# A one-core transformer layer with an expert feed-forward: more expert tiles computed ahead of the dense stage, and four smaller moves in the order of its engines

## The chip, the cores and the metric

The kernel runs on one core of a Trainium2 chip. The metric is the device time of one execution in microseconds (us). Three runs of the kernel before gave 1698.33, 1704.1 and 1705.66 us; their median, 1704.1 us, is the time before. The engines are named as in the profile: PE is TensorE (matmuls), PEld its weight load, DVE is VectorE, ACT is ScalarE, POOL is GpSimd, SP is SyncE, which issues transfers.

## The reference, cut to what matters

One layer works on 512 latent tokens of width 1024. Differential attention gives `h`, a layer norm of the residual follows, and then comes a product-key expert network with 16384 experts:

```
h = layer_norm(DN_ALPHA * h + g1 * o, ln_g[0], ln_b[0])
u = h * (1 + sc2) + sh2
q = (u @ w_q).reshape(T, 8, 2, 128)              # 8 heads, 2 halves
s = einsum('thcd,ckd->thck', q, sub_keys)        # key scores, 128 keys per half
s1, i1 = top_k(s[:, :, 0], 16);  s2, i2 = top_k(s[:, :, 1], 16)
top_s, pos = top_k(all 256 sums s1 + s2, 16)     # the 16 chosen experts idx of each head
g = softmax(top_s)
act = gelu(einsum('thkd,td->thk', u_tab[idx], u))
f = einsum('thk,thkd->td', g * act, v_tab[idx])
h = layer_norm(DN_ALPHA * h + g2 * f, ln_g[1], ln_b[1])
```

## The kernel before, in words

Tokens stand in four blocks of 128. Blocks 0, 1 and 2 (`DT = 3`) are computed densely: all 16384 experts are taken, as 128 tiles of 128 experts, and an expert that a token did not choose gets the gate 0. Block 3 is computed sparsely: the 128 chosen rows of `u_tab` and the 128 chosen rows of `v_tab` of each token are gathered by POOL and multiplied up on DVE (`fetch`, `gather`, `some`). All large products are float32 by three matmuls: each operand is split by ACT into a rounded part (`hi`) and by DVE or POOL into the rest (`lo`), and `mm3` issues hi·hi, hi·lo and lo·hi (lines 146, 148 and 149).

From the product-key part on, the stages are these.

- **Key scores** (`scores`): 16 rounds. Each splits one block of `w_q` (`qhi` on ACT, `qlo` on POOL), multiplies it with `u` (24 matmuls), multiplies with the keys (4 matmuls), and DVE takes the top 16 of four blocks (`top16`). In the last round there is no product, and one expert tile is computed instead.
- **Choices** (`choose`, `decide`): for each block DVE finds the 16 best of the sums, turns positions into expert numbers, and the softmax of the gates takes one exponential (`gg`) on ACT, line 961. Blocks 3, 0 and 1 come here one after the other. In between, PE computes expert tiles ahead: `ahead(n, rows)` splits a tile of `u_t` (`split_up`: `ur` is loaded by SP, `uhi` is made on ACT, `ulo` on POOL), makes 24 matmuls over blocks 0 to 2 (`up`, tile `a`), and ACT takes the GELU of them into `at`; `ad` in DRAM holds the results until they are needed. Splits run up to three tiles ahead of the matmuls. `rows` of the sparse block are gathered beside them; three of these stay `HOLD`-en before DVE uses them.
- **Gates** (`onehot`, `gates`): for each of the blocks 0 to 2, eight steps. DVE builds one-hot tiles `o`, `oh`, `ol`, 32 small matmuls spread the gates over all experts, ACT copies them to `w`, SP stores them in DRAM (`gd`). Each step also computes two expert tiles ahead (`WITH_GATES`), with `ulo` on DVE. The choice of block 2 stands behind the eight steps of block 0.
- **Dense stage** (`down`): for each of the 128 tiles `prepare` loads `v_t` (`vr`, two tiles in one transfer on ACT's queue), the stored `at` (`ar`) and gates (`gq`), and splits them: `vh`, `wh` on ACT, `vl`, `w`, `wl` on DVE; 18 matmuls add the tile to six accumulators. `prepare` runs two tiles ahead. Tiles that were not computed ahead ("fresh" ones) get their `up` here, six tiles before their use. At its end the rows of block 3 are complete and `finish` makes the last norm; for that `residual` loads the normalized state `nd`, and POOL multiplies with `ln_g` and adds `ln_b` (lines 1221 and 1222). Blocks 0 to 2 are finished after the last five tiles.

The order on each engine is that of a scheduler, which may move an instruction when it is free to, except for what goes through `Pinned` (`self.V`, `self.A`, `self.T`): those stand in the order of the program, and in the profile they all have line 97. `SPILL = 44` makes 90 tiles computed ahead. `WITH_CHOICE` lists by block how many tiles stand beside its choice, and how many gathered rows: (9, 0) for block 3, (9, 5), (11, 6), (9, 5) for blocks 0, 1, 2.

Of the kernel before, what the change touches and what calls it, by code (L numbers as in the profile page):

```python
# [31 lines left out]
SPILL = 44  # L32


WITH_CHOICE = {DT: (9, 0), 0: (9, 5), 1: (11, 6), 2: (9, 5)}
# [67 lines left out]
class Net:  # L103
# [5 lines left out]
    def build(self):  # L109
        with ExitStack() as es:  # L110
# [6 lines left out]
            self.T = Pinned(self, self.nc.tensor)  # L117
            self.consts()
# [539 lines left out]
    def mix(self):  # L658
# [8 lines left out]
        self.nd = self.dram.tile([NT, 128, D], F32, name="nd")  # L667
        self.keys = self.u2p.tile([128, 2, 128], F32, name="keys")
# [182 lines left out]

# [3 lines left out]
    def scores(self):  # L855
# [4 lines left out]
        with tc.tile_pool(name="qp", bufs=1, reuse_waits="tile") as qp:  # L860
# [17 lines left out]
            def split(k):  # L878
                if k < 2 * H:
                    S[k] = [qp.tile([128, KB, 128], FR, name=x, bufs=2) for x in ("qhi", "qlo")]  # L880
                    self.A.activation(S[k][0], RAW[k], AF.Copy)
                    (nc.vector if k < 4 else nc.gpsimd).tensor_tensor(S[k][1], RAW[k], S[k][0].bitcast(F32), op=OP.subtract)  # L882
# [11 lines left out]
            for k in range(2 * H):  # L894
# [4 lines left out]
                elif k:  # L899
                    self.ahead(1)  # L900
                ps = self.bank()
# [7 lines left out]
                if k == 1:  # L909
# [8 lines left out]
                    self.ug = tc.alloc_tile_pool(name="ug", bufs=1, side="right", reuse_waits="tile")  # L918

# [16 lines left out]
    def decide(self, t, h0, h1):  # L936
# [24 lines left out]
        self.A.activation(g, g, AF.Exp)  # L961
# [27 lines left out]
        V.tensor_reduce(by_head(self.i2f), m, axis=AX.X, op=OP.add)  # L989
        yield 1  # L990
# [140 lines left out]
    def down(self):  # L1131
# [7 lines left out]
        def prepare(j, at_end=None):  # L1139
# [14 lines left out]
            self.hi_lo(vh, vl, vq[j // 2][:, j % 2])  # L1154
# [3 lines left out]
            nc.vector.tensor_tensor(w.rearrange("p (q t) -> p q t", t=32), gq[j // 8][:, :, j % 8],  # L1158
                                    self.AT[j // 2][:, j % 2].rearrange("p (q t) -> p q t", t=32), op=OP.mult)
            self.prepared = self.hi_lo(wh, wl, w)  # L1160
# [3 lines left out]
        for j in fresh:  # L1164
            if j < AHEAD:
                self.up(j)
        prepare(0)
        prepare(1)
# [11 lines left out]
        for j in range(128 - TM):  # L1180
            if at(j - 1) == 256 and not row:
                row += self.last_rows()
                skip[DT] = self.residual(self.ag.tile([128, D], F32, name="gr", bufs=5), DT, row)
# [14 lines left out]
        for t in range(DT):  # L1198
            skip[t] = self.residual(fp.tile([128, D], F32, name="h", bufs=3), t, row)
# [9 lines left out]
    def last_rows(self):  # L1209

        row = []
        for n in range(4):
# [104 lines left out]
```

## Time and profile before

| what | value |
|---|---|
| runs of the kernel before | 1698.33, 1704.1, 1705.66 us |
| time of the profiled execution | 1702.72 us |
| its span, first to last instruction | 1700.9 us |
| mean granted TensorE clock | 0.98 of full speed |
| busy: PE, DVE, ACT, POOL | 1608.8, 1462.5, 761.8, 646.2 us |
| moved by DMA | 435.92 MB, 256 GB/s on average |

The product-key part begins at about 425 us of the span, the choices at 528 us, the first gates at 683 us, the last gates end at 963.7 us, the first dense step starts at 992.5 us. A busy share says how long an engine had work in it, not whether the work was on the path that ended last; what counts here is where PE stood idle, and for whom it waited. In a row of the waits, "PE v L146 <- ACT wh L138: 9.8, 2, 8.8" is read as: the matmuls of line 146 into tile `v` waited for ACT's tile `wh` (line 138), 9.8 us in total, twice, 8.8 us at most. In a timeline row the brackets hold the idle time of the engine just before, and who ended it. Rows of stretches give, for each engine, busy time and (in brackets) the number of instructions, then the granted clock, the busy share of the DMA engines, and GB/s.

### The profile page before, as it was taken

Reading aid. Unit: us, or ns where it says so; the run is one execution under the profiler, and the core shown is the slowest. Engines: PE = TensorE matmul, PEld = TensorE weight load, DVE = VectorE, ACT = ScalarE, POOL = GpSimd, SP = SyncE. Lnnn points to the kernel's source line nnn. Section 1 sums busy time; section 2 is a strip of 40 time slices with the busy share of each in tenths; the row PEclk is TensorE's granted clock in tenths of the full one; section 3 lists DMA queues with packets and bytes.
Section 4 is the critical chain, followed back from the end, with each engine's and each line's share of the span. In section 5 each row is a group of like instructions: output and inputs, shape, how many; then the busy total and the mean of one; then the engine's idle time right before and its main releaser. Section 6 shows DMA issues by size and latency. Waiting matters only on the chain.

```text
span 1700.9 us, 24498 instructions
## 1 busy us (share of the span) xinstructions
PE 1608.8 (95%) x9057; PEld 1430.2 (84%) x9057; DVE 1462.5 (86%) x2598; ACT 761.8 (45%) x1148; POOL 646.2 (38%) x368
## 2 busy tenths in 40 slices
PE   7899999997999999899999979999999999999977
PEld 3788897876888998899999968888888888888865
DVE  6688897887799999999999468989899789888978
ACT  5475656654333343564666533333333333333322
POOL 1000000000234676327333235655566556655552
PEclk9999999998999999899999989999999999999988
DMA  8765746403222566798999999989899889988952
GB/s 317 192 173 153 180 130 177 151 21 127 89 86 73 177 224 206 266 347 266 333 367 340 331 359 360 378 319 374 322 376 360 336 331 372 362 333 296 356 193 97
DMA packets 134920, 435.92 MB, mean 256 GB/s; under 512 B 13200, under 2 KB 38288, under 8 KB 123408
## 3 DMA queue, kind: packets, MB, share of 16 engines
q1 hardware_dynamic: 75328, 201.02, 34.7%
q0 software_dynamic: 36864, 134.23, 21.2%
q10 hardware_dynamic: 22608, 99.10, 16.6%
q8 instruction: 71, 1.16, 0.3%
q14 instruction: 49, 0.40, 0.1%
HBM read 372.57 MB, written 47.05 MB: 247 GB/s over the span
## 4 chain that ended last, share of the span: by engine, by line
PE 77%; DVE 9%; DMA 6%; issue 4%; ACT 2%; POOL 2%; SPq 0%; ACTq 0%; DVEq 0%; POOLq 0%
PE v L149 11%; PE v L146 10%; PE v L148 10%; PE a L149 10%; PE a L146 10%; PE a L148 9%; PE v L97 3%; PE qkv L146 2%; PE qkv L149 2%; PE qkv L148 2%; DMA adw<-in_ada_b_dram 2%; PE sc L409 2%; DMA qs<-kh 1%; PE mp L228 1%; POOL ulo L1019 1%
## 5 line engine op out<-in xcount | busy, mean ns | idle before, releaser
L146 PE MATMUL a<-u2h,uhi 128*128 128x384 f32 x1024 | 346.7, 339 | 4.5 <-ACT at L97 2.8
L149 PE MATMUL a<-u2h,ulo 128*128 128x384 f32 x1024 | 344.9, 337 | 6.2 <-POOL ulo L1019 4.5
L148 PE MATMUL a<-u2l,uhi 128*128 128x384 f32 x1024 | 343.9, 336 | 0.0
L146 PE MATMUL v<-vh,wh 128*128 128x512 f32 x768 | 300.9, 392 | 9.8 <-ACT wh L138 9.8
L148 PE MATMUL v<-vl,wh 128*128 128x512 f32 x768 | 301.7, 393 | 8.1 <-DVE vl L139 8.1
L149 PE MATMUL v<-vh,wl 128*128 128x512 f32 x768 | 301.7, 393 | 4.6 <-DVE wl L139 4.5
L1095 POOL DMA_INDIRECT gr<-in_peer_u_dram,eidx x128 | 184.3, 1440 | 242.4 <-DVE gr L1104 226.6
L1019 POOL TENSOR_TENSOR ulo<-ur,uhi 128x1024 fp32r<-128x1024 f32 x79 | 210.2, 2666 | 124.2 <-ACT uhi L97 70.1
L138 ACT ACTIVATE vh<-vr 128x1024 fp32r<-128x1024 f32 x128 | 134.6, 1054 | 237.6 <-DMA vr<-in_v_t_dram 96.7
L1095 POOL DMA_INDIRECT gr<-in_peer_v_dram,eidx x128 | 183.1, 1431 | 150.0 <-DVE facc L1111 129.8
L139 DVE TENSOR_TENSOR vl<-vr,vh 128x1024 fp32r<-128x1024 f32 x128 | 164.5, 1286 | 70.6 <-ACT vh L138 70.6
L882 POOL TENSOR_TENSOR qlo<-qraw,qhi 128x1024 fp32r<-128x1024 f32 x12 | 28.8, 2401 | 465.2 <-ACT qhi L97 465.2
L149 PEld LDWEIGHTS a<-u2h,ulo 128*128 128x128 f32 x1024 | 193.2, 189 | 8.5 <-POOL ulo L1019 6.5
L146 PEld LDWEIGHTS a<-u2h,uhi 128*128 128x128 f32 x1024 | 193.3, 189 | 7.1 <-ACT at L97 3.7
L148 PEld LDWEIGHTS a<-u2l,uhi 128*128 128x128 f32 x1024 | 193.4, 189 | 1.5
L1111 DVE SCALAR_TENSOR_TENSOR facc<-gr,act,facc 128x1024 f32<-128x1024 f32 x127 | 184.6, 1453 | 6.1 <-DMA gr<-in_peer_v_dram,eidx 6.1
L146 PEld LDWEIGHTS v<-vh,wh 128*128 128x128 f32 x768 | 145.4, 189 | 39.9 <-ACT wh L138 10.5
L148 PEld LDWEIGHTS v<-vl,wh 128*128 128x128 f32 x768 | 145.6, 190 | 38.6 <-DVE vl L139 8.8
L149 PEld LDWEIGHTS v<-vh,wl 128*128 128x128 f32 x768 | 145.3, 189 | 36.5 <-DVE wl L139 5.9
L97 ACT ACTIVATE at<-a 128x384 f32<-128x384 f32 x90 | 44.2, 492 | 184.7 <-PE a L149 111.3
L139 DVE TENSOR_TENSOR wl<-w,wh 128x384 fp32r<-128x384 f32 x128 | 93.1, 728 | 23.9 <-ACT wh L138 23.5
L138 ACT ACTIVATE wh<-w 128x384 fp32r<-128x384 f32 x128 | 65.1, 517 | 106.7 <-PE v L148 65.7
(269 smaller groups left out, 3257.4 us busy)
## 6 DMA issues: line engine op xcount, KB each, us to landing
ur<-in_u_t_dram SPq DMA_DIRECT2D x128, 512.0 KB, 5.8
vr<-in_v_t_dram ACTq DMA_DIRECT2D x64, 1024.0 KB, 8.2
gq<-gd SPq DMA_DIRECT2D x16, 1536.0 KB, 12.3
gd<-w SPq DMA_DIRECT2D x12, 1920.0 KB, 8.9
ad<-at SPq DMA_DIRECT2D x45, 384.0 KB, 6.3
ar<-ad SPq DMA_DIRECT2D x45, 384.0 KB, 7.3
adw<-in_ada_b_dram ACTq DMA_DIRECT2D x64, 256.0 KB, 3.5
wraw<-in_w_qkv_dram ACTq DMA_DIRECT2D x21, 512.0 KB, 4.2
```

The lines of the kernel that those rows point to most:

```text
L97: ins = getattr(self.engine, name)(*args, **kwargs)
L138: (hi_engine or nc.scalar).activation(hi, src, AF.Copy)
L139: return (lo_engine or nc.vector).tensor_tensor(lo, src, hi.bitcast(F32), op=OP.subtract)
L146: ins = nc.tensor.matmul(out, lh, rh, start=first and i == 0, stop=False)
L148: nc.tensor.matmul(out, lh, rl, start=False, stop=False)
L149: ins = nc.tensor.matmul(out, ll, rh, start=False, stop=last and i == n - 1)
L228: nc.tensor.matmul(mp[:2, 2 * i + n], l[:, kb], r[:, ns], start=kb == 0 and k == 0, stop=kb == KB - 1 and k == 2)
L409: nc.tensor.matmul(ps[:, c, n0:n1], QS[h, c][:, v, t * 128:(t + 1) * 128], KS[h, c][:, n0:n1], start=v == 0, stop=v == 1)
L882: (nc.vector if k < 4 else nc.gpsimd).tensor_tensor(S[k][1], RAW[k], S[k][0].bitcast(F32), op=OP.subtract)
L1019: self.paced = (lo_engine or self.nc.gpsimd).tensor_tensor(lo, raw, hi.bitcast(F32), op=OP.subtract)
L1095: ins = nc.gpsimd.indirect_dma_start(out=self.GR[n], out_offset=None, in_=a["peer_v"] if n >= K else a["peer_u"], in_offset=bass.IndirectO ...
L1111: ins = nc.vector.scalar_tensor_tensor(self.facc, r, self.act[:, k:k + 1], self.facc, op0=OP.mult, op1=OP.add)
```

## The change

Five things are edited.

1. `SPILL` goes from 44 to 48: the formula in `spilled` now picks 98 tiles to compute ahead, and 30 are left fresh in the dense stage (38 before). `WITH_CHOICE` becomes (10, 0), (11, 3), (14, 3), (9, 3): one, two and three tiles more beside the choices of blocks 3, 0 and 1, and five rows less by the end of block 1, two less beside block 2. Five tiles instead of three are left over behind the last gates; 199 instead of 192 rows are left to the dense stage.
2. The exponential of each choice is issued later on ACT: after the expert numbers are complete instead of right after the differences are formed. Two tiles' GELUs and splits that stood behind it now stand ahead.
3. The splits of the first three tiles are issued in rounds 13, 14 and 15 of the key scores instead of all in round 15 (`split_ahead`).
4. `prepare(0)` and `prepare(1)` are pinned on DVE and ACT, as are tiles of `up` ahead of them (none is there with either value of `SPILL`).
5. `residual` no longer multiplies and adds. Rounds 5 to 12 of the key scores do that on POOL, in one step a round, each behind the round's `qlo`; rounds 3, 5, 7 and 9 load `nd`, and POOL's own queue writes the result to `hd`. The end loads `hd`. `qlo` is pinned on POOL from tile 4 on, so that these steps stand between.

```diff
-SPILL = 44
-WITH_CHOICE = {DT: (9, 0), 0: (9, 5), 1: (11, 6), 2: (9, 5)}
+SPILL = 48
+WITH_CHOICE = {DT: (10, 0), 0: (11, 3), 1: (14, 3), 2: (9, 3)}
...
+            self.P = Pinned(self, self.nc.gpsimd)
...
     def ahead(self, n, rows=0, lo_engine=None):
-        for i in range(n):
-            while len(self.ready) < min(self.done + 3, len(self.early)):
-                j = self.early[len(self.ready)]
-                self.ready.append(self.split_up(j, self.A, lo_engine))
+        for i in range(min(n, len(self.early) - self.done)):
+            self.split_ahead(self.done + 3, lo_engine)
...
+    def split_ahead(self, n, lo_engine=None):
+        while len(self.ready) < min(n, len(self.early)):
+            self.ready.append(self.split_up(self.early[len(self.ready)], self.A, lo_engine))
...
-                    (nc.vector if k < 4 else nc.gpsimd).tensor_tensor(S[k][1], RAW[k], S[k][0].bitcast(F32), op=OP.subtract)
+                    (nc.vector if k < 4 else self.P).tensor_tensor(S[k][1], RAW[k], S[k][0].bitcast(F32), op=OP.subtract)
...
+                if k > 2 * H - 4:
+                    self.split_ahead(k - 2 * H + 4)
...
+                    row, skip = self.rows(0), []
+                if 3 <= k < 13:
+                    t, step = divmod(k - 5, 2)
+                    if k in (3, 5, 7, 9):
+                        skip.append(self.ag.tile([128, D], F32, name="gr", bufs=5))
+                        nc.sync.dma_start(skip[-1], self.nd[len(skip) - 1])
+                    if k > 4:
+                        self.P.tensor_tensor(skip[t], skip[t], row[step], op=(OP.mult, OP.add)[step])
+                        if step:
+                            self.P.dma_start(self.hd[t], skip[t])
...
         V.tensor_tensor(g, top, top[:, :, 0:1].to_broadcast([128, N, TK]), op=OP.subtract)
         yield 1
-        self.A.activation(g, g, AF.Exp)
...
         V.tensor_reduce(by_head(self.i2f), m, axis=AX.X, op=OP.add)
+        self.A.activation(g, g, AF.Exp)
         yield 1
...
-        prepare(0)
-        prepare(1)
+        prepare(0, vector=self.V, act=self.A)
+        prepare(1, vector=self.V, act=self.A)
...
-    def residual(self, h, t, row):
-        nc = self.nc
-        nc.sync.dma_start(h, self.nd[t])
-        nc.gpsimd.tensor_tensor(h, h, row[0], op=OP.mult)
-        nc.gpsimd.tensor_tensor(h, h, row[1], op=OP.add)
+    def residual(self, h, t):
+        self.nc.sync.dma_start(h, self.hd[t])
         return h
```

How this moves instructions is read from the built programs at three places. The first is ACT in the choice of block 3; `uhi` is the split of an expert tile, `at` its GELU, `gg` the exponential, and a table load stands at each change between GELU and exponential. Before:

```order
L97 ACTIVATE uhi_5588<-ur_5586 128x1024
L97 ACTIVATE at_5549<-a_5592 128x384
L97 ACTIVATE uhi_5622<-ur_5620 128x1024
L97 ACTIVATE at_5626<-a_5627 128x384
L97 ACT_TABLE_LOAD
L97 ACTIVATE gg_4497<-gg_4497 128x128
L97 ACTIVATE uhi_5665<-ur_5663 128x1024
L97 ACT_TABLE_LOAD
L97 ACTIVATE at_5626<-a_5669 128x384
```

The same place now:

```order
L97 ACTIVATE uhi_5689<-ur_5687 128x1024
L97 ACTIVATE at_5651<-a_5693 128x384
L97 ACTIVATE uhi_5722<-ur_5720 128x1024
L97 ACTIVATE at_5726<-a_5727 128x384
L97 ACT_TABLE_LOAD
L97 ACTIVATE gg_4498<-gg_4498 128x128
L97 ACTIVATE uhi_5769<-ur_5767 128x1024
L97 ACT_TABLE_LOAD
L97 ACTIVATE at_5726<-a_5773 128x384
```

The neighbours look alike; what moved is the count ahead of `gg`: five GELUs of expert tiles (one from the key scores, four of this choice) before, seven now.

The second is ACT at the start of the dense stage; the first `vr` holds tiles 0 and 1 of `v_t`, the second tiles 2 and 3, each `vh` and `wh` belongs to one dense step. Before:

```order
L1143 DMA vr_10136<-in_v_t_dram 128x2048
L97 ACTIVATE at_10069<-a_10096 128x384
L1143 DMA vr_10162<-in_v_t_dram 128x2048
L138 ACTIVATE vh_10142<-vr_10136 128x1024
L138 ACTIVATE vh_10152<-vr_10136 128x1024
L138 ACTIVATE vh_10166<-vr_10162 128x1024
L138 ACTIVATE wh_10147<-w_10146 128x384
```

And now:

```order
L1161 DMA vr_10430<-in_v_t_dram 128x2048
L1036 ACTIVATE uhi_10535<-ur_10533 128x1024
L97 ACTIVATE at_10337<-a_10338 128x384
L1036 ACTIVATE uhi_10601<-ur_10599 128x1024
L97 ACTIVATE at_10337<-a_10364 128x384
L97 ACTIVATE vh_10410<-vr_10404 128x1024
L97 ACTIVATE wh_10415<-w_10414 128x384
L97 ACTIVATE vh_10420<-vr_10404 128x1024
L139 ACTIVATE vh_10434<-vr_10430 128x1024
L1161 DMA vr_10500<-in_v_t_dram 128x2048
L97 ACTIVATE wh_10425<-w_10424 128x384
```

The `wh` of step 0 stood behind the first `vh` that needs the second `vr`; it now stands behind the first `vh` of the first `vr`. Two more GELUs stand between the loads and the first `vh`. The `wh` of step 1 still stands behind the `vh` of step 2.

The third is POOL in the key scores; `gr` is here a block of the normalized state with the `ln_g` or `ln_b` row. Before:

```order
L882 TENSOR_TENSOR qlo_4813<-qraw_4696,qhi_4812 128x1024
L882 TENSOR_TENSOR qlo_4873<-qraw_4756,qhi_4872 128x1024
L882 TENSOR_TENSOR qlo_4933<-qraw_4816,qhi_4932 128x1024
L882 TENSOR_TENSOR qlo_4993<-qraw_4876,qhi_4992 128x1024
L882 TENSOR_TENSOR qlo_5053<-qraw_4936,qhi_5052 128x1024
```

And now:

```order
L97 TENSOR_TENSOR qlo_4820<-qraw_4701,qhi_4819 128x1024
L97 TENSOR_TENSOR gr_4757<-gr_4757,gr_4633 128x1024
L97 TENSOR_TENSOR qlo_4883<-qraw_4763,qhi_4882 128x1024
L97 TENSOR_TENSOR gr_4757<-gr_4757,gr_4635 128x1024
L97 DMA hd_4144<-gr_4757 128x1024
L97 TENSOR_TENSOR qlo_4945<-qraw_4823,qhi_4944 128x1024
L97 TENSOR_TENSOR gr_4879<-gr_4879,gr_4633 128x1024
L97 TENSOR_TENSOR qlo_5008<-qraw_4886,qhi_5007 128x1024
```

One step of the norm's affine part stands behind each `qlo`, and behind each second one of these a transfer on POOL's queue; at the end of the kernel the eight steps of lines 1221 and 1222 are gone.

More of the change, by code (lines that the diff above doesn't have):

```diff
@@ L667, in mix @@
         self.nd = self.dram.tile([NT, 128, D], F32, name="nd")
+        self.hd = self.dram.tile([NT, 128, D], F32, name="hd")
         self.keys = self.u2p.tile([128, 2, 128], F32, name="keys")
@@ L1137, in down, with prepare @@
         gq, vq, ready = {}, {}, {}
-        def prepare(j, at_end=None):
+        def prepare(j, at_end=None, vector=nc.vector, act=nc.scalar):
             if j % 2 == 0:
@@ L1153, in prepare @@
             vl = pool.tile([128, D], FR, name="vl", bufs=bufs)
-            self.hi_lo(vh, vl, vq[j // 2][:, j % 2])
+            self.hi_lo(vh, vl, vq[j // 2][:, j % 2], vector, act)
             w = vp.tile([128, TD], F32, name="w", bufs=2)
@@ L1157, in prepare @@
             wl = pool.tile([128, TD], FR, name="wl", bufs=bufs)
-            nc.vector.tensor_tensor(w.rearrange("p (q t) -> p q t", t=32), gq[j // 8][:, :, j % 8],
+            vector.tensor_tensor(w.rearrange("p (q t) -> p q t", t=32), gq[j // 8][:, :, j % 8],
                                     self.AT[j // 2][:, j % 2].rearrange("p (q t) -> p q t", t=32), op=OP.mult)
-            self.prepared = self.hi_lo(wh, wl, w)
+            self.prepared = self.hi_lo(wh, wl, w, vector, act)
             ready[j] = wh, wl, vh, vl
@@ L1181, in down @@
             if at(j - 1) == 256 and not row:
-                row += self.last_rows()
-                skip[DT] = self.residual(self.ag.tile([128, D], F32, name="gr", bufs=5), DT, row)
+                row += self.rows(1)
+                skip[DT] = self.residual(self.ag.tile([128, D], F32, name="gr", bufs=5), DT)
                 self.finish(self.ag, row, skip, DT, [self.facc[:, :512], self.facc[:, 512:]])
@@ L1198, in down @@
         for t in range(DT):
-            skip[t] = self.residual(fp.tile([128, D], F32, name="h", bufs=3), t, row)
+            skip[t] = self.residual(fp.tile([128, D], F32, name="h", bufs=3), t)
         for t in range(DT):
@@ L1207, in down, with rows @@
         ap.release()
-    def last_rows(self):
+    def rows(self, i):
         row = []
-        for n in range(4):
+        for n in (2 * i, 2 * i + 1):
             row.append(self.ag.tile([128, D], F32, name="gr", bufs=5))
-            self.nc.sync.dma_start(row[n], self.a["ln"][n:n + 1].to_broadcast([128, D]))
+            self.nc.sync.dma_start(row[-1], self.a["ln"][n:n + 1].to_broadcast([128, D]))
         return row
-    def residual(self, h, t, row):
-        nc = self.nc
-        nc.sync.dma_start(h, self.nd[t])
-        nc.gpsimd.tensor_tensor(h, h, row[0], op=OP.mult)
-        nc.gpsimd.tensor_tensor(h, h, row[1], op=OP.add)
+    def residual(self, h, t):
+        self.nc.sync.dma_start(h, self.hd[t])
         return h
```

10 lines of the change are left out of this document (5 added, 5 removed).

## The prediction

> **What bounds the kernel now.** I read the busy times by stage first, then the waits of PE, then the timeline around each long wait. These are the stages from the key scores on: key scores, choices, gates, the way to the first dense step, dense steps, the end.
>
> ```profile
> 425.00:528.40 103.40, 102.13 (x539) 86.24 (x538) 87.28 (x428) 34.23 (x51) 28.81 (x12) 1.00 0.23 73
> 528.40:683.20 154.80, 140.53 (x797) 137.19 (x796) 148.47 (x372) 60.77 (x83) 101.94 (x45) 0.98 0.59 191
> 683.20:963.70 280.50, 279.05 (x2095) 274.91 (x2095) 260.09 (x335) 172.05 (x211) 103.78 (x60) 0.98 0.92 324
> 963.70:992.50 28.80, 19.97 (x117) 19.65 (x114) 4.07 (x5) 10.46 (x14) 6.70 (x4) 0.94 0.92 356
> 992.50:1642.60 650.10, 647.35 (x3031) 559.26 (x3031) 567.82 (x625) 230.46 (x316) 376.93 (x231) 0.99 0.92 345
> 1642.60:1700.90 58.30, 35.95 (x144) 28.31 (x143) 49.55 (x82) 11.88 (x19) 20.01 (x10) 0.84 0.22 79
> ```
>
> The first number behind the comma is PE's busy time. In the gates PE is busy 279.05 of 280.50 us, in the dense steps 647.35 of 650.10: there PE sets the pace, and work taken from it is time. In the choices it stands idle 154.80 - 140.53 = 14.3 us, on the way to the first dense step 28.80 - 19.97 = 8.8 us, and at the end another share. DVE is fuller than PE in the choices alone (148.47 of 154.80): there it is the bound. These are the waits of PE from 528 us on:
>
> ```profile
> PE v L146 <- ACT wh L138: 9.8, 2, 8.8
> PE v L148 <- DVE vl L139: 8.1, 1, 8.1
> PE v L97 <- DVE o L97: 5.1, 1, 5.1
> PE a L149 <- POOL ulo L1019: 4.5, 3, 1.8
> PE v L149 <- DVE wl L139: 4.5, 2, 2.7
> PE a L146 <- ACT at L97: 2.8, 3, 1.6
> PE a L146 <- ACT uhi L97: 1.7, 1, 1.7
> PE a L149 <- DVE ulo L97: 1.5, 1, 1.5
> ```
>
> Each is a single place, so the list is short: 38 us in all. The 4.5, 2.8, 1.7 and 5.1 us lie in the choices (14.1 us together), the 1.5 at the first gates, the 8.8 before the first dense step, one 2.7 soon after it, and 8.1 + 1.8 + 1.0 near the end. Around a long wait the granted clock is cut as well:
>
> ```profile
> 683.00:686.00 3.00, 2.83 (x27) 0.50 0.00 1
> 690.00:694.00 4.00, 4.00 (x19) 0.76 0.65 177
> 1650.00:1654.00 4.00, 1.40 (x3) 0.50 0.00 0
> 566.00:572.00 6.00, 4.64 (x26) 1.00 0.46 135
> ```
>
> The clock behind the 5.1 us wait is half until about 692 (0.76 from 690 to 694), and half behind the 8.1 us wait; behind the short waits at 566 us it is whole. From 683.2 to 691.9 less the 1.5 us wait are 7.2 us at half clock, 3.6 us lost. By the same length I estimate 2.6 us at the end and 1.8 us behind the 8.8 us wait: 8 us. So the whole that can be won here is 38 + 8 = 46 us. The tiles moved ahead win nothing by themselves: PE has the same matmuls to do. They win by standing where PE waits.
>
> **Term 1: the choices.** A tile costs PE this much:
>
> ```profile
> 539.86:564.90 25.04, 25.04 (x144) 1.00 0.41 132
> ```
>
> That is 25.04 x 24 / 144 = 4.17 us. Six tiles more stand ahead of the first gates (1 + 2 + 3): 25.0 us. If PE no longer waits, the stage takes 140.5 + 25.0 = 165.5 us and the gates start at 693.9 instead of 683.2. Of the 14.3 us of idle time I leave 1.5: gain 12.8 us. Three reasons. First, DVE: it is late by 5.1 us now, and PE arrives 10.7 us later. DVE has five gathered rows less, but POOL has six splits more beside it:
>
> ```profile
> L1104 DVE SCALAR_TENSOR_TENSOR gr<-gr,row 128x1024 f32<-128x1024 f32 x8 | 9.5, 1213 | 0.0
> ```
>
> ```profile
> 611.58 5.32 DVE L97 TENSOR_TENSOR bb<-pb 128x128 bf16<-128x128 bf16 x1
> ```
>
> ```profile
> 612.05 4.76 POOL L1019 TENSOR_TENSOR ulo<-ur,uhi 128x1024 fp32r<-128x1024 f32 x2
> ```
>
> Five rows are 5 x 9.5 / 8 = 5.9 us less. Against that, an operation on only 128 elements took DVE 5.32 us while POOL made two splits in 4.76 us: DVE stood still for them. Six more splits cost DVE between 0 (beside the top 16) and 6 x 4.76 / 2 = 14.3 us. Its first one-hot comes between 677.3 and 691.6 us, against PE's 693.9: it is covered over the whole range, by 2.3 us at the worst end. The Trainium skill has a rule for this ("SBUF — State Buffer", section "SBUF: two separate sides"): a DVE operation with two SBUF inputs and a GpSimd one that reads SBUF take a shared port pair in turn, and the one that comes second waits for the whole of the first. By it the six splits cost at most their own length, which is the same upper end; it speaks against putting tiles here, and the trace agrees with its sign.
>
> Second, the exponential:
>
> ```profile
> 562.70 0.31 ACT L97 ACTIVATE gg<-gg 128x128 f32<-128x128 f32 x1 [4.07 <-DVE gg L97]
> ...
> 565.27 0.49 ACT L97 ACTIVATE at<-a 128x384 f32<-128x384 f32 x1
> ```
>
> ACT stood 4.07 us for DVE's `gg`, with a GELU and the splits behind it; PE then ran out of a free result bank (2.8 us over three choices) and of `ulo` (two of the three waits of 4.5). Two tiles, 8.3 us, now stand ahead of it, so ACT reaches it that much later and the wait is gone, or under 1 us in block 3. The new wait that it can make is DVE's, for the softmax sum behind it: PE starts block 3's tiles near 534 us (528.4, one tile and the last key matmuls) and ends the sixth of block 0's choice near 534 + 16 x 4.17 = 601 us, while DVE is still at block 0's expert numbers at 611.58 (row above), ahead of the sum. Nothing. Third, the first splits: PE waited 1.7 us for `uhi` and 1.8 for `ulo` since all three splits were issued behind the last scores; three rounds earlier they are ready. Loading them costs nothing, since the key scores move only 73 GB/s.
>
> **Term 2: the norm's affine part in the key scores.** POOL has this there, and at the end the second row:
>
> ```profile
> L882 POOL TENSOR_TENSOR qlo<-qraw,qhi 128x1024 fp32r<-128x1024 f32 x12 | 28.8, 2401 | 465.2 <-ACT qhi L97 465.2
> ```
>
> ```profile
> L1222 POOL TENSOR_TENSOR h<-h,gr 128x1024 f32<-128x1024 f32 x3 | 8.5, 2822 | 0.2
> ```
>
> ```profile
> L1095 POOL DMA_INDIRECT gr<-in_peer_u_dram,eidx x13 | 15.7, 1207 | 7.7 <-DVE gr L1104 5.6 <-issue 1.1 <-DVE gh L97 0.3
> ```
>
> A round is about 103.4 / 16 = 6.5 us. POOL takes 2.4 + 2.8 = 5.2 us of it, in each second round a transfer besides; such an issue is not in the trace, but an indirect one takes POOL 1.2 us. Two rounds need 11.6 of 13 us: hidden, 0 us. If the issue took over 2.6 us, `qlo` would come late, by up to 1 us in four rounds: 0 to 4 us. On SP the fourth `nd` load must wait for the first `hd` to be written, since it takes that buffer, and five `qraw` loads are queued behind it; a load is asked for two rounds, 13 us, before the split that reads it, so I take 0 again, and up to 3 us for the range.
>
> **Term 3: the clock and the gates.** With the 5.1, 8.8 and 8.1 us waits gone or short, the half clock goes: 8 us. The 1.5 us wait for `ulo` came from DVE being late: 1.4 us.
>
> **Term 4: the first dense step.** PE has 142 tile matmuls between the last gate and the first dense one in the built program, 114 before: 28 x 0.174 = 4.9 us more, so it arrives at 963.7 + 19.97 + 4.9 = 988.6 us on the old scale. The inputs:
>
> ```profile
> 986.20 2.00 ACT L138 ACTIVATE vh<-vr 128x1024 fp32r<-128x1024 f32 x2 [9.29 <-DMA vr<-in_v_t_dram]
> 990.99 1.06 ACT L138 ACTIVATE vh<-vr 128x1024 fp32r<-128x1024 f32 x1 [2.78 <-DMA vr<-in_v_t_dram]
> ...
> 991.95 0.51 ACT L138 ACTIVATE wh<-w 128x384 fp32r<-128x384 f32 x1
> ```
>
> `wh` stood behind a `vh` that waited for the second `vr` until 990.99. In the new order ACT is free for it at 988.2; DVE's `vl` and `w` must come first, for which I allow 1.3 us: `wh` ends near 989.9. PE waits 1.3 us instead of 8.8: gain 7.5 us. If the first `vr` lands no earlier, that is the floor of this wait. Of the 2.7 us wait behind it (a slow `vl`, beside two splits of POOL) I take half: 1.4 us.
>
> **Term 5: the dense steps.** 6 + 28 / 24 = 7.17 tiles, 29.9 us, are gone from the 650.1 us, and seven rows are added:
>
> ```profile
> L1111 DVE SCALAR_TENSOR_TENSOR facc<-gr,act,facc 128x1024 f32<-128x1024 f32 x127 | 184.6, 1453 | 6.1 <-DMA gr<-in_peer_v_dram,eidx 6.1
> ```
>
> ```profile
> DVE vl L139 <- ACT vh L138: 48.3, 34, 4.4
> DVE wl L139 <- ACT wh L138: 22.9, 23, 2.5
> ```
>
> DVE needs 567.8 + 7 x 1.45 = 578 of 650.1 - 29.9 + 2 - 1.4 = 620.8 us, 93%; now it is 87%. Its idle time is 71 us of waiting for ACT, and ACT waits for buffers that PE frees; so far it has room. Runs of seven steps without a fresh tile become the rule. I take 2 us of new waits here, between 0 and 10.
>
> **Term 6: the end.**
>
> ```profile
> 1641.87 5.57 DVE L1233 SCALAR_TENSOR_TENSOR gr<-gr,gf 128x512 f32<-128x512 f32 x2 [4.76 <-POOL gr L1222]
> ...
> 1648.56 2.16 DVE L139 TENSOR_TENSOR vl<-vr,vh 128x1024 fp32r<-128x1024 f32 x1
> ```
>
> DVE stood for POOL's affine steps, and the `vl` that PE waited 8.1 us for was queued behind. The steps are gone; only a load of `hd` is left. What is late next is the splitting of the last three tiles, which can't begin before PE frees their buffers: I leave 2 of 10.9 us. Gain 8.9 us. What follows the last matmul is unchanged.
>
> **Sum.** 12.8 + 8 + 1.4 + 7.5 + 1.4 + 8.9 - 2 = 38 us. Against the profiled execution, 1702.7 - 38 = 1664.7 us; the median of the runs is 1.4 us above it, so **1666 us**. If no wait is left anywhere it is 8 us less, and as the clock's share may be larger I put the lower end at 1653. Its own range is 1653 to 1676.
>
> **The rivals.**
>
> *DVE still sets the pace in the choices* (chance 0.10). The splits fall differently and cost DVE 10 us beyond my upper end of 691.6. PE waits some 8 us at the first gates and half clock follows: 1676 us. For it: DVE is 96% busy there. Against it: five rows less, and a margin over the whole bound. It decides from 2.3 us beyond that end.
>
> *Transfers set the pace of the dense steps* (0.12). They move 650.1 x 0.345 = 224.3 MB; eight `u_t` tiles less, four stored pairs and seven rows more make 225.3 MB in 620.8 us, 363 GB/s.
>
> ```profile
> 1148.00:1173.00 25.00, 25.00 (x119) 1.00 1.01 409
> ```
>
> Against it: 409 GB/s were moved for 25 us without a wait of PE. For it: never for a stage. At 355 GB/s the steps take 634.7 us: +14, 1680 us. It decides below 363. The Trainium skill ("SBUF — State Buffer", section "A bandwidth-pool intuition that's wrong (but worth ruling out)") gives HBM to one core as about 358 GB/s; by that the steps would take 629 us and the whole 1674. The row above is higher than its figure.
>
> *DVE's chain, not PE, sets the dense steps* (0.03). Then its 650.1 us don't shrink, the seven rows add 10.2, and `vl` is late at the end as it is now: 1666 + 39.5 + 8.9 = 1714 us, slower than before. It decides when a DVE step with its waits stays above 620.8 / 120 = 5.2 us (650.1 / 120 = 5.4 now). Against it: those waits end with ACT, and ACT's with PE.
>
> *The same with the end repaired* (0.03): about 1705 us, no change.
>
> **How the numbers follow.** The forecast has 0.72, the others 0.28. About 0.5% (8.5 us) is what a measurement of this kernel can tell from no change. The forecast and the first two rivals are all faster by more: 0.94. No change 0.03, slower 0.03. The range takes in the forecast's own, the first rival and most of the second: 1653 to 1684 us.
>
> **What would show it.** In the waits of PE after the change: no `o`, no `at`, `ulo` under 2 us, one short `wh` in the place of the 8.8, no `vl` of 8 us; clock 1.00 at the first gates; gates starting 8 to 13 us later than 683.2, dense steps some 28 us shorter than 650.1. I am wrong if PE's busy share in the dense steps falls below 98%, if a wait for `qlo` shows in the key scores, or if a wait for `o` remains.

## The result and the profile after

The kernel after takes 1663.1 us (median of 4 runs, 1658.1 to 1666.3), the kernel before 1704.2 us (median of 4 runs there): 41 us less, ratio 0.976, 95% interval 0.973 to 0.980, faster. Forecast was 1666 us in 1653 to 1684. The profiled execution is the slowest of the four; it spans 1664.6 us against 1700.9, 36.3 us less, and 37.8 us less from the choices on, which start 1.5 us later in it. 38 were forecast.

These are the stages of the kernel after, cut at the places that correspond to those of before: key scores, choices, gates, the way to the first dense step, dense steps, end. The columns are the stretch, its length, the busy time of PE, its weight loads, DVE, ACT and POOL, the granted clock, the DMA share, and GB/s.

```profile
425.00:529.90 104.90, 103.63 (x547) 87.74 (x547) 88.52 (x432) 35.05 (x52) 52.53 (x25) 0.99 0.36 125
529.90:693.00 163.10, 161.51 (x939) 160.64 (x938) 154.94 (x371) 68.16 (x93) 115.23 (x46) 1.00 0.59 187
693.00:968.50 275.50, 275.50 (x2096) 271.89 (x2096) 247.17 (x321) 172.51 (x212) 104.15 (x59) 1.00 0.93 328
968.50:995.00 26.50, 24.75 (x144) 24.43 (x142) 5.46 (x5) 11.23 (x16) 4.80 (x2) 1.00 0.99 372
995.00:1620.20 625.20, 619.14 (x2859) 528.94 (x2860) 548.55 (x657) 223.65 (x305) 355.71 (x227) 0.99 0.95 362
1620.20:1664.60 44.40, 33.13 (x145) 26.74 (x143) 34.48 (x65) 10.92 (x17) 7.74 (x5) 0.90 0.27 98
```

In the choices PE is idle 163.1 - 161.5 = 1.6 us, where it was 14.3, and the stage is 8.3 us longer, since it holds six tiles more. The gates have neither a wait nor a cut clock and are 5.0 us shorter. The way to the first dense step is 2.3 us shorter with 28 tile matmuls more in it. The dense steps are 24.9 us shorter, but 6 us of waiting stand in them now, where there were under 3. At the end the stretch is 13.9 us shorter. All waits of PE from the choices on:

```profile
PE v L150 <- DVE wl L140: 4.5, 4, 2.6
PE v L147 <- ACT wh L97: 1.8, 1, 1.8
PE a L150 <- POOL ulo L1037: 1.4, 1, 1.4
PE v L147 <- ACT wh L139: 1.2, 1, 1.2
PE a L147 <- ACT at L97: 0.2, 1, 0.2
```

They are 9.1 us in place of 38; the waits for `o` and, at the end, for `vl` are gone. The single places are `ulo` at 571 us (1.4), `wh` at 995 (1.8, before the first dense step), `wl` at 1014 (2.6), and four from 1097 to 1175 us (0.8, 0.4, 1.2, 0.8). From there to the last matmul PE does not wait at all.

### The profile page after: what moved, and what is told of

It is laid out like the page before. It is cut to its first block, busy times and chain, and to the rows that moved or that the text cites. A ratio compares the mean times of both kernels' runs of the same rounds, so it can differ in the third digit from the quotient of the medians.

```text
span 1664.6 us, 24509 instructions
## 1 busy us (share of the span) xinstructions
PE 1601.1 (96%) x9057; PEld 1423.8 (86%) x9057; DVE 1423.3 (86%) x2600; ACT 763.6 (46%) x1148; POOL 647.7 (39%) x370
## 3 DMA queue, kind: packets, MB, share of 16 engines
q1 hardware_dynamic: 77056, 206.26, 36.3%
## 4 chain that ended last, share of the span: by engine, by line
PE 73%; DVE 9%; DMA 8%; issue 5%; POOL 3%; ACT 1%; SPq 0%; DVEq 0%; ACTq 0%; POOLq 0%
PE a L147 10%; PE a L150 10%; PE a L149 10%; PE v L150 9%; PE v L149 9%; PE v L147 9%; PE v L97 4%; DMA adw<-in_ada_b_dram 3%; DMA gr<-in_peer_u_dram,eidx 2%; PE qkv L150 2%; PE qkv L147 2%; PE qkv L149 2%; PE sc L410 2%; POOL gr L1113 1%; PE mp L229 1%
## 5 line engine op out<-in xcount | busy, mean ns | idle before, releaser
L1113 POOL DMA_INDIRECT gr<-in_peer_u_dram,eidx x128 | 188.1, 1469 | 247.8 <-DVE gr L1122 233.7
L140 DVE TENSOR_TENSOR vl<-vr,vh 128x1024 fp32r<-128x1024 f32 x126 | 158.3, 1257 | 35.8 <-ACT vh L139 34.3
L1129 DVE SCALAR_TENSOR_TENSOR facc<-gr,act,facc 128x1024 f32<-128x1024 f32 x127 | 171.3, 1349 | 4.9 <-DMA gr<-in_peer_v_dram,eidx 4.8
L97 ACT ACTIVATE at<-a 128x384 f32<-128x384 f32 x98 | 48.2, 492 | 203.0 <-PE a L150 102.7
L140 DVE TENSOR_TENSOR wl<-w,wh 128x384 fp32r<-128x384 f32 x126 | 81.4, 646 | 27.5 <-ACT wh L139 26.5
```

The lines of the kernel that those rows point to most:

```text
L97: ins = getattr(self.engine, name)(*args, **kwargs)
L140: return (lo_engine or nc.vector).tensor_tensor(lo, src, hi.bitcast(F32), op=OP.subtract)
L1113: ins = nc.gpsimd.indirect_dma_start(out=self.GR[n], out_offset=None, in_=a["peer_v"] if n >= K else a["peer_u"], in_offset=bass.IndirectO ...
L1129: ins = nc.vector.scalar_tensor_tensor(self.facc, r, self.act[:, k:k + 1], self.facc, op0=OP.mult, op1=OP.add)
```

## The experiments

Every run is compared with the kernel before, in runs on its own chip; the whole change is worth 41 us there (a repeat of the kernel after, below, gave ratio 0.975, interval 0.973 to 0.978). How much slower than the kernel after a run is, I take from the difference of the two ratios. Two ratios whose intervals overlap I call not told apart.

**The tile counts alone.** The kernel before, with two constants of the change.

```diff
-SPILL = 44
+SPILL = 48
-WITH_CHOICE = {DT: (9, 0), 0: (9, 5), 1: (11, 6), 2: (9, 5)}
+WITH_CHOICE = {DT: (10, 0), 0: (11, 3), 1: (14, 3), 2: (9, 3)}
```

> The kernel before with the new tile counts alone (96 tiles ahead, 10 + 11 + 14 + 9 of them and 9 rows beside the choices); everything else is as before. Theory (each wait is paid at its own place, and the tiles repair only those that DVE's lateness makes): the 5.1 us wait for o, the 1.5 us for ulo at the first gates and 3.6 us of half clock go, some 10 us; the waits for uhi, ulo and at in the choices (9 us), the 8.8 us before the first dense step and the 10.9 us at the end stay, and 3 us of new waits come in the dense steps: 1695 us, between 1690 and 1699, ratio to the kernel before 0.994 to 0.998. Rival (the tile counts are nearly the whole change and the other parts decoration): 1665 to 1672 us. In the trace the theory expects a wait of over 6 us for vl near the end and one for wh of over 4 us before the first dense step.

1680.6 us, ratio 0.987 (0.985 to 0.990): 22 us faster than before. Both theories missed. (With `SPILL = 48` 98 tiles are ahead, not the 96 of the expectation.) Its longest waits of PE:

```profile
PE v L148 <- DVE vl L139: 7.8, 1, 7.8
PE v L146 <- ACT wh L138: 4.1, 1, 4.1
PE a L149 <- POOL ulo L1019: 3.2, 2, 1.8
```

The end kept its waits, as my theory said. But the choices lost more than the `o` (`at` 2.8 became 0.7, `ulo` 4.5 became 3.2, and 1.5 at the first gates went), and the wait before the first dense step fell from 8.8 to 4.1 us with no line of its order changed. Only 1.0 us of that is work: 120 tile matmuls stand between the last gate and the first dense step here, 114 before. The step itself comes 25.0 us behind the last gate in place of 28.7: the transfers that it waits for land earlier against the gates, and why they do is not shown.

**All but the tile counts.** The kernel after with those two constants put back.

> The kernel after with the old tile counts (88 tiles ahead, 9 + 9 + 11 + 9 and 16 rows beside the choices); the other parts stay. Theory (DVE sets the pace of the choices once six tiles are missing, so that the short waits repaired on ScalarE and by the early splits only make the wait for o longer): gates start at 683 to 686 us, PE idle in the choices 11 to 15 us in spite of the repaired waits, half clock behind it: 13 to 18 us slower than the kernel after, 1676 to 1681 us. Rival (each part pays by itself): only the 5.1 + 1.5 us waits and 3.6 us of half clock come back, less some 3 us of dense waits: 1670 to 1673 us. In the trace: a wait for o of 9 to 14 us by the theory, 5 us by the rival.

1684.0 us, ratio 0.989 (0.986 to 0.991): 18 us faster than before, 21 slower than after. Its two longest waits:

```profile
PE v L97 <- DVE o L97: 9.2, 1, 9.2
PE v L147 <- ACT wh L97: 6.0, 1, 6.0
```

The theory holds for the choices in part. The waits there for `uhi`, `ulo` and `at` fell from 9.0 to 1.6 us by the repairs on ScalarE and the early splits, but the `o` wait grew from 5.1 to 9.2 us and took 4.1 of these 7.4 back. What I had not expected is the 6.0 us before the first dense step: that stretch has its fixed order here too. The two halves, 22 and 18 us, make 40 of the 41 us.

**The affine part back at the end.** The rows and the two GpSimd operations go back from the key scores to `last_rows` and `residual`, as in the kernel before.

```diff
-                    row, skip = self.rows(0), []
-                if 3 <= k < 13:
...
-        self.nc.sync.dma_start(h, self.hd[t])
+        nc.sync.dma_start(h, self.nd[t])
+        nc.gpsimd.tensor_tensor(h, h, row[0], op=OP.mult)
+        nc.gpsimd.tensor_tensor(h, h, row[1], op=OP.add)
```

> The kernel after with the norm's affine part back at the end (four rows loaded there, two GpSimd operations for each block, nothing of it beside the key scores). Theory: DVE stands for GpSimd's two operations again and the vl of the last tiles is queued behind it; a wait of 7 to 9 us for vl, 1 to 2 us more, and 2.6 us of half clock: 9 to 12 us slower than the kernel after, 1672 to 1676 us. Rival (with the new counts DVE has so much room at the end that it hides the two operations): within 2 us of the kernel after. If the key scores had a hidden price for the affine part (the upper end of term 2), they would be up to 4 us shorter here; theory: no change there.

1677.0 us, ratio 0.984 (0.981 to 0.986): some 13 us slower than after, a little more than the theory had. Near its end, on DVE, and the wait of PE that follows:

```profile
1616.23 5.59 DVE L1240 SCALAR_TENSOR_TENSOR gr<-gr,gf 128x512 f32<-128x512 f32 x2 [2.29 <-POOL gr L1229]
...
1622.95 2.16 DVE L140 TENSOR_TENSOR vl<-vr,vh 128x1024 fp32r<-128x1024 f32 x1
```

```profile
PE v L149 <- DVE vl L140: 7.7, 1, 7.7
...
PE v L150 <- DVE fm L652: 1.8, 1, 1.8
```

It is the picture of the kernel before, and the waits are 9.5 us. The clock is 0.50 from 1622.0 to 1632.2 us; PE works 5.2 us of that, so the half clock costs 2.6 us more. Together 12.1. In the key scores PE waits the same 0.7 and 0.5 us with the affine part there and without: it costs nothing.

**Without the fixed order before the first dense step.**

```diff
-                self.up(j, self.split_up(j, self.A), self.A)
-        prepare(0, vector=self.V, act=self.A)
-        prepare(1, vector=self.V, act=self.A)
+                self.up(j)
+        prepare(0)
+        prepare(1)
```

> The kernel after without the fixed order on the way to the first dense step (the first fresh tiles and the first two prepared tiles go where the scheduler puts them: ScalarE then splits the second and third v tile ahead of the first wh). Theory (the order was what made the 8.8 us wait): the wait before the first dense step grows from 1.8 to between 5 and 9 us, with half clock behind it: 4 to 8 us slower than the kernel after. Rival (the 28 tile matmuls that now stand there gave the transfers time to land; the wait ends with the load of gates or of stored tiles, whatever the order): within 1 us of the kernel after, the wait between 1 and 3 us.

1661.0 us, ratio 0.976 (0.974 to 0.979): the same as the kernel after. The rival's time came, but not by its reason; the wait is as long as the theory had it:

```profile
PE v L147 <- ACT wh L139: 5.5, 1, 5.5
PE a L150 <- POOL ulo L1037: 1.4, 1, 1.4
```

One wait of 5.5 us stands for the 1.8 + 2.6 + 3.2 us of the kernel after. ScalarE's rows there:

```profile
983.54 1.06 ACT L139 ACTIVATE vh<-vr 128x1024 fp32r<-128x1024 f32 x1 [6.54 <-DMA vr<-in_v_t_dram]
...
988.81 1.06 ACT L139 ACTIVATE vh<-vr 128x1024 fp32r<-128x1024 f32 x1 [2.89 <-DMA vr<-in_v_t_dram]
989.78 0.51 ACT L139 ACTIVATE wh<-w 128x384 fp32r<-128x384 f32 x1
```

`wh` stands behind a third `vh` that waits for its transfer, just as I had read it before the change. But the first dense step starts 26.4 us behind the last gate here, and 26.5 in the kernel after. What the fixed order does is to put 22 matmuls of one more tile in front of it (142 in place of 120, 3.8 us), and these fill most of the longer wait. Without it three tiles are split when PE starts, and PE does not wait again for 50 us; that the one is the reason for the other is my reading, no run separates it. The order moves the wait, it doesn't remove it.

**The exponential at its old place.** One line moved back, behind the first `yield 1` after `gg`.

> The kernel after with the exponential at its old place in the order, two tiles earlier. Theory: ScalarE stands for DVE's gg again in each block (4 us or more in blocks 3 and 0), PE runs out of result banks and of ulo: waits for at and ulo of 4 to 6 us together in the choices, where now is one of 1.4 us; 3 to 5 us slower than the kernel after. Rival (with more tiles the exponential is reached later anyway, and DVE is the one that is late): within 1 us.

1672.1 us, ratio 0.984 (0.983 to 0.986): some 14 us slower than after, by far more than the theory. ScalarE, first in this run, then in the kernel after:

```profile
562.39 0.31 ACT L97 ACTIVATE gg<-gg 128x128 f32<-128x128 f32 x1 [11.82 <-DVE gg L97]
```

```profile
566.26 0.31 ACT L97 ACTIVATE gg<-gg 128x128 f32<-128x128 f32 x1 [3.55 <-DVE gg L97]
```

DVE has `gg` when its top 16 are done, and the place of the exponential doesn't move that: it is 128.3 us after the first matmul of the key scores in both. With the early splits PE makes its tiles some 5 us earlier than in the kernel before, so ScalarE comes to the exponential 5 us earlier; DVE's `gg` comes 2 us later than there, and ScalarE stands for it 11.8 us in place of 4.1. PE waited 8.5 us for `at`, and 1.0 for `ulo`. Its clock was 0.50 from 562.0 to 572.2 us, and PE worked 5.7 us of that: 2.9 us more. The kernel with the tile counts alone, which has neither the early splits nor the later exponential, waits 5.6 us in its choices and loses 1.7 us to the clock; this one, with the early splits, 9.5 and 2.9. The early splits need the later exponential.

**Without the early splits.** The `split_ahead` during the last key scores is taken out.

> The kernel after without the early splits of the first three tiles during the last key scores. Theory: waits of 1.7 us for uhi and about 1.8 us for ulo come back at the start of the choices, 3 to 4 us slower than the kernel after; since DVE then has 3 us more room, nothing else changes. Rival (DVE still sets the choices, so PE only waits at another place): within 1 us, and a wait for o appears.

1664.0 us, ratio 0.980 (0.978 to 0.981): not told apart from the kernel after. In its trace the 1.7 us for `uhi` and 1.8 for `ulo` are back at the start of the choices and the 1.4 us at 571 are gone, a difference of 2.1 us; the clock is 0.50 behind them for 3.4 us, some 1.5 more; no wait for `o` came. The size is under what the run times resolve, but not under what the traces do: from the first matmul of the key scores to the first of the gates PE takes 258.3 us here, and between 255.0 and 255.1 us in four traces of the same code with the early splits (the kernel after, its repeat, the run without the fixed order, and the one with more traffic). So they save 3.2 us, as the theory had it. The same stretch takes 261.1 us with neither the early splits nor the later exponential (the tile counts alone, with the affine part at the end), and 265.5 us with the early splits only: the splits lose 4.4 us there.

**More rows beside the choices.**

```diff
-WITH_CHOICE = {DT: (10, 0), 0: (11, 3), 1: (14, 3), 2: (9, 3)}
+WITH_CHOICE = {DT: (10, 0), 0: (11, 8), 1: (14, 8), 2: (9, 8)}
```

> The kernel after with 24 gathered rows beside the choices in place of 9, so 15 fewer in the dense steps. It measures by how much DVE is ahead of the gates. By the trace of the kernel after DVE ends the second step's one-hots some 10 us before PE needs the first. 15 rows by 1.2 us are 18 us more of DVE. Theory (margin 8 to 10 us): a wait for o of 7 to 11 us and 2 to 4 us of half clock, while 15 rows fewer leave the dense steps 1 to 3 us shorter: 6 to 13 us slower than the kernel after. Rival (the margin is the 2.3 us that the prediction's worst end left): a wait of 14 us or more, 14 to 20 us slower. Second rival (the rows lie in DVE's gaps while it waits for nothing else): no wait for o.

1665.1 us, ratio 0.979 (0.978 to 0.981): not told apart, and no wait for `o`; the second rival is right. DVE's first one-hots in the kernel after (PE needs them at 693.0 us), then here (693.9):

```profile
668.37 1.22 DVE L97 TENSOR_TENSOR o<-iota,ii 128x2048 f16<-128x2048 f16 x1
...
670.77 3.43 DVE L97 TENSOR_TENSOR ol<-o,gl 128x2048 f16<-128x2048 f16 x1
674.12 4.54 DVE L97 TENSOR_TENSOR o<-iota,ii 128x2048 f16<-128x2048 f16 x2
```

```profile
684.38 1.21 DVE L97 TENSOR_TENSOR o<-iota,ii 128x2048 f16<-128x2048 f16 x1
...
689.99 2.35 DVE L97 TENSOR_TENSOR o<-iota,ii 128x2048 f16<-128x2048 f16 x2
```

15 rows put DVE 16 us later and PE still found its one-hots ready: they end by 692.4 at the latest. In the kernel after the four end by 678.7, so DVE is at least 14 us ahead, not 10 (I had read the second step's set) and not 2. What came instead is waits for `ulo` in the gates, 0.7 and 2.0 us.

**A load held back.** The exponential one tile later still, and the second load of gates (1.5 MB) behind the stored tiles' loads.

```diff
+                if j:
+                    self.behind(ins, self.loaded)
...
-        self.A.activation(g, g, AF.Exp)
         yield 1
+        self.A.activation(g, g, AF.Exp)
```

> A try at what is left: the kernel after with the exponential one tile later still, and with the second load of gates (1.5 MB for the dense steps 8 to 15), which the scheduler had put among the first loads of the dense steps, held behind the loads of the stored tile pairs up to there. Theory (the waits of 1.8 and 2.6 us at the first dense steps end with transfers, at 391 GB/s between 974 and 1002 us; 1.5 MB less there are 3.9 us): both waits shrink to under 1.5 us together, the 1.4 us wait for ulo in the choices goes: 3 to 4.5 us faster than the kernel after, about 1659 us. Rival (the loads that are waited for stand ahead of it in the queue anyway): only the 1.4 us go. A second rival: the gates land late for step 8, a new wait there.

1674.5 us, ratio 0.984 (0.981 to 0.987): slower than after by some 13 us (its profiled execution, at 1668.6 us, is one of the quicker ones, and its waits account for that one). The first half did what it should: from 530 to 690 us PE is busy 160.00 of 160 us. The second half made another wait of 4.1 us before the first dense step; ScalarE there:

```profile
992.72 1.06 ACT L1036 ACTIVATE uhi<-ur 128x1024 fp32r<-128x1024 f32 x1 [4.95 <-DMA ur<-in_u_t_dram]
993.68 0.51 ACT L97 ACTIVATE wh<-w 128x384 fp32r<-128x384 f32 x1
```

With the load gone from its place the scheduler put `u_t` loads there and a `uhi` that waits for one ahead of `wh`. So the run says what a `uhi` in the wrong place costs, and nothing on the transfer that it was made for. More waits (2.9, 1.7, 1.6 us) came further on.

**The kernel after again.**

> The kernel after once more, unchanged, on the same chip as the three beside it, so that differences of a few us between them can be read: 1660 to 1666 us, ratio to the kernel before 0.975 to 0.979. Its waits from the key scores on are the same ones at the same places if they belong to the program and not to the execution.

1661.3 us, ratio 0.975 (0.973 to 0.978). The same places: 1.4 us at 572, 1.2 at 995, 2.6 at 1014, and 0.3, 0.9, 0.8 between 1157 and 1173. They belong to the program. What differs is the start: PE's first matmul of the key scores comes between 433 and 440 us in these traces, with the same code in front of it. That is what limits how finely run times can be compared here, and why a stretch that begins at that matmul tells more.

**More traffic.** 20 copies of 0.52 MB within memory; the reading end is the first part of a stored block of gates.

```diff
+            if j in range(8, 48, 2):
+                nc.sync.dma_start(self.sd[j // 2], self.gd[0].rearrange("p q j t -> p (q j t)")[:, :1024])
```

> The kernel after with 20 additional copies of 0.52 MB from memory to memory, one in each second dense step from 8 to 46, that nobody waits for; the order of all other instructions is the same on every engine. It tells whether transfers set the pace of the first third of the dense steps, where the kernel after has its new waits. Theory 1 (transfers: the stretch runs at 350 to 390 GB/s and the most that was seen over 25 us is 409 GB/s): 10.5 MB more have no room; at 400 GB/s they take 26 us, of which 5 to 15 us fit in, so 10 to 20 us slower than the kernel after, with waits of PE for splits that waited for v tiles. Theory 2 (DVE's and ScalarE's order sets it, transfers have room): within 3 us of the kernel after.

1668.0 us, ratio 0.981 (0.978 to 0.983). The experiment missed its place: that part of the gates is stored early, and SyncE sent the copies between 775 and 860 us, in the gates. The dense steps have the waits of the kernel after, so on them it says nothing. Where they landed it says something. From 750 to 850 us the DMA share is 0.98 (0.86 in the kernel after) and PE is busy 93.56 us of 100 (100.00 there). ScalarE in that stretch:

```profile
845.76 0.49 ACT L97 ACTIVATE at<-a 128x384 f32<-128x384 f32 x1 [9.52 <-DMA ad<-at]
```

A store of tile results came late, ScalarE stood 9.5 us for the buffer that this store frees, and PE waited 6.4 us for ScalarE's copies `w` behind it, with 2 us of clock; measured are 7 to 9 us.

**Rows by PE's work.** Two tries at a better kernel, both with the later exponential; the second also without the fixed order.

```diff
-        at = lambda i: min(n0 + (256 - n0) * max(i, 0) // 116, 256)
+        work = [0]
+        for j in range(128 - TM):
+            work.append(work[-1] + 1 + (j + AHEAD in fresh))
+        at = lambda i: min(n0 + (256 - n0) * work[max(i, 0)] // work[116], 256)
```

> A try at a better version: the kernel after with the exponential one tile later (it took the last wait out of the choices in an earlier run) and with the gathered rows of the dense steps handed out by PE's work in place of by steps: a step that also makes a fresh tile lasts 8.3 us and gets two shares, one without 4.1 us and one share. Theory (in runs of six steps without a fresh tile DVE and the transfers are asked for more than PE's time, since each step has the same 1.7 rows; with 1.4 they are not): the four waits of 3.2 us between 1090 and 1180 us go, and the 1.4 us in the choices: 3 to 5 us faster than the kernel after. Rival (the steps that now get three rows put vl behind them on DVE, and wait there): new waits for vl of 2 us or more, no gain or a loss.

> The same with the scheduler's own order on the way to the first dense step. Theory (the fixed order only moves the wait, as the run without it showed: 5.5 us at the first step and none behind it, against 1.8 + 2.6 + 3.2 us with it): within 2 us of the run with paced rows, one wait of 5 to 6 us at the first step. Rival (with paced rows nothing is left for the delay to repair): 3 to 5 us slower than it, by the longer wait and the half clock behind it.

1665.9 us, ratio 0.979 (0.976 to 0.982), and 1658.4 us, ratio 0.973 (0.970 to 0.976). The first has no gain. Its dense waits:

```profile
PE v L150 <- DVE wl L140: 5.2, 3, 2.6
PE v L149 <- DVE vl L140: 4.4, 1, 4.4
```

The rival is right in its result: the four waits between 1090 and 1180 us are gone, but 1.8 us stand at 1028, 1.4 around 1200, and a `vl` at 1245 us waits 4.4 us behind a row of which DVE waited 5.4 us for the transfer. The second is 2.8 us faster than the repeat beside it, with overlapping intervals: not told apart from the kernel after. Against the first it is 7.5 us faster, which neither expectation had, with intervals that only just touch. It has two waits left, 5.5 us for `wh` at the first dense step and 1.9 us for a `vl`.

## Why the prediction was right, and where not

**Term 1, choices (12.8 us forecast):** idle time went from 14.3 to 1.6 us, 12.7. The mechanism is shown from both sides: with the old counts the `o` wait returns at 9.2 us, with 15 rows more it still doesn't. Two steps of the working were off. DVE's first one-hots were to be ready between 677.3 and 691.6 us; by the rows above they are ready between 676 and 679, so what the splits cost DVE was at the low end, and the cover is 14 us, not 2.3. Single rows do show DVE and GpSimd in each other's way: `ol` took 3.43 us beside a split of 3.36, against 1.22 alone. That is as the shared-port rule of the Trainium skill has it ("SBUF — State Buffer", "SBUF: two separate sides"). But the upper bound, all of the six splits' length, never came near; why so little of it fell on DVE is not shown. And of the exponential I said that ScalarE's wait is gone "or under 1 us in block 3": it is 3.55 us there, and PE's 1.4 us at 571 comes from it (a tile later, it is gone). That the exponential is worth some 14 us next to the early splits was in no step.

**Term 2, affine part (0):** 0. POOL's operations and its stores in the key scores:

```profile
L97 POOL TENSOR_TENSOR qlo<-qraw,qhi 128x1024 fp32r<-128x1024 f32 x12 | 28.8, 2400 | 444.7 <-ACT qhi L97 444.7
L97 POOL TENSOR_TENSOR gr<-gr 128x1024 f32<-128x1024 f32 x8 | 19.1, 2384 | 0.0
L97 POOL DMA_DIRECT2D hd<-gr x4 | 2.6, 640 | 1.2 <-PE v L97 1.2
```

2.4 us for 2.8 and 0.64 for 1.2: both estimates from rows of another kind were on the safe side. The 0.5 us that PE waits there for a `qlo` of DVE are in the kernel before as well.

**Term 3, clock and gates (8 + 1.4):** these are the stretches of half clock from the choices to the last matmul, five in the kernel before, then two in the kernel after (length, busy time of PE, clock, DMA share, GB/s):

```profile
534.90:538.30 3.40, 3.40 (x12) 0.51 0.73 235
681.70:691.90 10.20, 7.28 (x43) 0.50 0.22 73
988.90:995.70 6.80, 3.19 (x8) 0.50 1.02 423
1012.80:1016.20 3.40, 3.40 (x10) 0.50 0.74 227
1647.70:1657.90 10.20, 5.30 (x12) 0.50 0.11 28
```

```profile
1013.90:1017.30 3.40, 3.40 (x8) 0.50 0.88 330
1174.30:1177.70 3.40, 3.25 (x8) 0.51 1.03 381
```

Half of PE's busy time in them is lost: 11.3 us before, 3.3 after, so the gain is the 8.0 us that were forecast. But it is made up otherwise. The forecast had the second, third and fifth stretch. It missed the first, behind the waits for `uhi` and `ulo` at 531 and 534 us, which is won too (1.7 us), and it had no term for the clock behind the new dense waits, where 1.6 us are lost at 1174. The gates show the term by itself: they hold as many matmuls as before (2096 and 2095 recorded) and are 5.0 us shorter, 1.5 of the wait for `ulo` and 3.5 of the clock.

**Term 4, first dense steps (7.5 + 1.4):** this step failed in its reason. The wait is 1.8 us where 1.3 was forecast, but not since `wh` could go earlier: the first dense step starts as far behind the last gate without the order, and with the order and the old counts the wait is 6.0 us. With the new counts and without the order it is 5.5 us, and from there to 1.8 it is one more tile in front. The sentence that failed is "In the new order ACT is free for it at 988.2; DVE's `vl` and `w` must come first, for which I allow 1.3 us: `wh` ends near 989.9". In the kernel after, on DVE, then what followed at the next wait, on DVE and on POOL:

```profile
993.88 0.56 DVE L97 TENSOR_TENSOR w<-gq,ar 128x384 f32<-128x384 f32 x1 [1.71 <-DMA ar<-ad]
...
1007.49 5.41 DVE L140 TENSOR_TENSOR vl<-vr,vh 128x1024 fp32r<-128x1024 f32 x1 [2.03 <-ACT vh L139]
```

```profile
1007.07 4.74 POOL L1037 TENSOR_TENSOR ulo<-ur,uhi 128x1024 fp32r<-128x1024 f32 x2
```

ScalarE was free; `w` waited for a transfer, and from 975 to 1000 us the transfers run at 397 GB/s and a DMA share of 1.02. And the 2.7 us behind it, of which I took half away, is 2.6: a `vl` of 5.4 us beside two splits of POOL.

**Term 5, new dense waits (2, 0 to 10):** 3.2 us, and 2.1 in the repeat. With the half clock behind them the dense steps take 625.2 us, 621.4 in the repeat, where 620.8 were forecast.

**Term 6, end (8.9):** no wait at all is left of 10.9, so the gain was 2 us larger. I had left 2 us for splits that wait for buffers; PE does not wait for them.

**Rivals.** DVE as the pace of the choices: no, by 14 us. That DVE is busy 95% of the choices still (154.94 of 163.10 us) shows that its busy share, on which I had called it the bound, was no proof. DVE's chain as the pace of the dense steps: no, they shrank. Transfers as their pace: not as a stage, which moves 362 GB/s over 625 us. The section of the Trainium skill that I cited gives a core 358. The page "Perfetto Trace Analysis" of the Trainium skill (section "Roofline") allows a core that runs alone about 435 GB/s; the 397 above, over 25 us, are over the first figure and under the second. In single places up to 1175 us a late `v` tile or row does stand ahead of PE's waits. Whether there is too much traffic there or only a bad order of it stays open: the run for it missed its place, the held load changed the order, and no other was made.

So the sum was right at 38 for 37.8 in the profiled execution and 41 in the medians, partly by luck. The choices gave 4 us more than forecast (8.3 us longer in place of 25.0 - 12.8 = 12.2) and the end 2.4 more (13.9 in place of 8.9 + 2.6); the dense steps gave 6 us less (625.2 us in place of 620.8 - 1.8, the clock behind the 8.8 us wait). The parts aren't independent: tiles make the room, the early splits are a loss without the later exponential and save 3 us with it, and the fixed order is worth nothing that could be measured.

## What to carry to other kernels

Work moved ahead pays where PE stands idle: list PE's waits by place, and add to each what half clock costs behind it. After an improvement, undo each part alone: here one part of five did nothing, and one was a loss without another. Where run times don't resolve a part, compare the stretch of the trace that it acts in, from a matmul that all kernels have in common. An order fixed by hand at a place where transfers come last moved the wait and didn't remove it; look at the next 100 us, not at the wait alone.

## What the runs showed of the hardware

How short a wait already cuts the clock. In all of these traces the cut clock is 0.50, and from the choices to the last matmul it lasts 3.4 us or two or three times as long (rows of term 3). Behind a wait of 2.0 to 2.9 us it came in eleven of thirteen places, and cost PE up to 1.7 us each time. At 1.4 us it is undecided: at the same wait for `ulo` the clock stayed whole in the kernel after and was cut in the run with the affine part at the end. And two waits of 2.6 us, in the run with more traffic and in the first with paced rows, left it whole. These are the first three of these places, in this order:

```profile
571.00:575.00 4.00, 3.64 (x21) 3.65 (x22) 3.96 (x3) 0.59 (x1) 4.00 (x3) 1.00 0.57 154
```

```profile
570.70:574.10 3.40, 3.40 (x13) 0.50 0.84 245
```

```profile
1016.00:1020.00 4.00, 3.94 (x18) 1.00 1.02 392
```

Of three waits of 1.8 to 1.9 us that stand alone one left the clock at 1.00 (at 995 us in the kernel after), two cut it (at 1028 and 1032 in the kernels with paced rows). So between 1.4 and 2.6 us the length of the wait alone does not decide; what does is not shown. Waits of 8.1 to 8.8 us cost 1.6 to 2.9 us more. The Trainium skill ("TensorE: Matmul & The Clock Gate", section "Why this matters for your kernels") warns of gaps over about 3 us. Here 2 us were mostly enough, so it is safer to count each wait of 2 us as 3.5.
